# Weighing and adding the even blocks on GpSimd in a mixture of softmaxes

## The chip, the cores and the metric

The kernel runs on one core of a Trainium2 chip. The metric is device time in microseconds (us), the median over the runs of a kernel. Engines are called by the names of the profile: PE is TensorE (PEld its weight loads), DVE is VectorE, ACT is ScalarE, POOL is GpSimd, SP is SyncE, which only issues transfers here.

## The reference

For each of 32·128 = 4096 rows there are 4 heads of 4096 logits and 4 prior values. Each head's logits go through a softmax, the priors go through a softmax over the 4 heads, and the output row is the sum of the four heads' softmaxes, each times its prior:

```
prior_probs = softmax(prior, axis=-1)          # [32, 128, 4]
softmax     = softmax(logits, axis=-1)         # [32, 128, 4, 4096]
mixture     = sum(prior_probs[..., None] * softmax, axis=2)   # [32, 128, 4096]
```

All data are 32-bit floats: 268 MB of logits in, 67 MB of mixture out.

## The kernel before

**Tiles.** A block `n` (of 64) holds 64 output rows. Its 128 partitions are 64 rows times two values of `x`, and a partition holds two heads, `y` = 0 and 1, of 4096 values each: 4 MB in one of five `ring` slots (block n in slot n mod 5). A unit `u` (of 32) is two blocks, the even block `e` = 2u and the odd block `o` = 2u+1, and gives 128 output rows. TensorE's sum goes to four `acc` tiles of PSUM (128 x 1024 each, all of PSUM); the even block's 64 rows are partitions 0 to 63 of `acc`, the odd block's are 64 to 127.

**Steps of a block.** `top(n, y)` (VectorE, L97) finds the negated maximum of each partition's 4096 values. `exp(n, y)` (ScalarE, L104) puts the exponentials in place of the logits and their sum into `dsum`. `weigh(n, y)` takes the reciprocal of the sum (VectorE, L110), and GpSimd multiplies a constant 128 x 64 matrix `mask` (a one where partition p belongs to row p // 2) by reciprocal and prior of the partition (L112): a small weight matrix `wt`. `mix(u, y)` (TensorE, L128) multiplies the exponentials of head half `y` with the weights; the two `x` of a row and, by accumulation in PSUM, the two `y` are summed. Eight column banks of 512, two blocks and two values of `y` make 32 matmuls a unit, which the trace shows as 64 instructions; even and odd block take turns. `drain` (ScalarE, L156) copies `acc` to an output buffer, and `store` (SP, L159) writes 2 MB.

**Order.** It is written out by hand and is the order of each engine's queue. For unit u, with e = 2u, o = 2u+1, the calls are:

```
top(e,0)  weigh(o-2,1)  half(u-1,1)  load(e+3) load(e+4)  top(e,1)
exp(e,0)  exp(e,1)  weigh(e,0)  top(o,0)  weigh(e,1)  top(o,1)
exp(o,0)  weigh(o,0)  drain(u-1)  store(u-1)  half(u,0)  exp(o,1)
```

`half(u, y)` is `mix` in units 0 to 27 (`FINE` = 28). In units 28 to 31 the blocks are cut otherwise: `half` is `pair` (L143), and GpSimd's weight matrices are 128 x 32 (L117). Whole blocks are loaded with L89, block 0 and those of units 28 to 31 in two halves with L94. The two loads of a unit go into the slots of the unit before, so they wait for the last matmul of `half(u-1, 1)`. All loads and stores are issued from SP's queue in this order. The stores of units 27 to 29 are held until unit 31.

Of the kernel before, what the change touches and what calls it, by code (L numbers as in the profile page):

```python
# [9 lines left out]
ALU = mybir.AluOpType  # L10
# [4 lines left out]
def kernel(  # L15
# [3 lines left out]
    prior: bass.AP,  # L19
    out: bass.AP,  # L20
):

# [5 lines left out]
    nc = tc.nc  # L30
# [3 lines left out]
    HP = P // 2  # L34
# [3 lines left out]
    RING = 5  # L38
    BANK = 512
    Q = 4  # L40
    W = V // Q
    HELD = 4
    FINE = U - 4
# [13 lines left out]
    ring = [cpool.tile([P, 2, V], FP32, name=f"ring{i}") for i in range(RING)]  # L57
    obuf = [cpool.tile([P, V], FP32, name=f"obuf{i}") for i in range(2)]
    acc = [psum.tile([P, W], FP32, name=f"acc{i}") for i in range(Q)]
# [4 lines left out]
    mask = cpool.tile([P, HP], FP32, name="mask")  # L64
    mask4 = cpool.tile([P, QP], FP32, name="mask4")
    pt = cpool.tile([P, 2, N], FP32, name="pt")
# [3 lines left out]
    rden = cpool.tile([P, N, 2], FP32, name="rden")  # L70
    wt = [
        [[cpool.tile([P, HP], FP32, name=f"wt{i}{b}{y}") for y in range(2)] for b in range(2)]
        for i in range(2)
    ]
# [33 lines left out]
    def weigh(n, y):  # L108
        w = wt[n // 2 % 2][n % 2][y]
        nc.vector.reciprocal(rden[:, n, y : y + 1], dsum[:, n, y : y + 1])  # L110
        if n < 2 * FINE:
            nc.gpsimd.tensor_scalar(  # L112
                out=w, in0=mask, scalar1=rden[:, n, y : y + 1],
                scalar2=pt[:, y, n : n + 1], op0=ALU.mult, op1=ALU.mult,
            )
        else:
            nc.gpsimd.tensor_scalar(  # L117
                out=w[:, :QP], in0=mask4, scalar1=rden[:, n, y : y + 1],
                scalar2=pt4[:, y, n - 2 * FINE : n - 2 * FINE + 1], op0=ALU.mult, op1=ALU.mult,
            )  # L120

    def mix(u, y):
        for q in range(Q):
            for k in range(W // BANK):
                for b in range(2):
                    n = 2 * u + b
                    c = q * W + k * BANK
                    nc.tensor.matmul(  # L128
                        acc[q][HP * b : HP * (b + 1), k * BANK : (k + 1) * BANK],
                        lhsT=wt[u % 2][b][y],  # L130
                        rhs=ring[n % RING][:, y, c : c + BANK],
                        start=y == 0,
                        stop=y == 1,
                    )

    def pair(u, b):
        n = 2 * u + b
        for q in range(Q):
            for k in range(W // BANK):
                for y in range(2):  # L140
                    g = 2 * b + y
                    c = q * W + k * BANK
                    nc.tensor.matmul(  # L143
                        acc[q][QP * g : QP * (g + 1), k * BANK : (k + 1) * BANK],
                        lhsT=wt[u % 2][b][y][:, :QP],
                        rhs=ring[n % RING][:, y, c : c + BANK],
                        start=True,
                        stop=True,
                        tile_position=(0, QP * g),
                    )  # L150
# [12 lines left out]
    with tc.manual_schedule():  # L163
# [42 lines left out]
        for u in range(U):  # L206
            e, o = 2 * u, 2 * u + 1
            if u:
                top(e, 0)
                weigh(e - 1, 1)  # L210
                half(u - 1, 1)
                load(e + RING - 2)
                load(e + RING - 1)
# [5 lines left out]
            exp(e, 0)  # L219
            exp(e, 1)  # L220
            weigh(e, 0)
            top(o, 0)
            weigh(e, 1)
            if u == LAST:
                for q in range(2):
# [50 lines left out]
```

## Time and profile before

| | us |
|---|---|
| median of 3 runs (787.76 to 787.88) | 787.78 |
| the profiled execution's own time | 787.68 |
| its span, first to last instruction | 786.0 |

| engine | busy us | share of the span |
|---|---|---|
| TensorE matmul | 514.7 | 65% |
| VectorE | 579.0 | 74% |
| ScalarE | 593.9 | 76% |
| GpSimd | 51.7 | 7% |

The 16 DMA engines move 335.97 MB, 427 GB/s over the span. A line of a group in the profile gives the line of code, the engine, the operation, what it writes from what it reads, shapes and count, then total busy us, mean ns of one, and the idle time of the engine ahead of it with what ended it. A line of the timeline gives start and duration in us and, in brackets, the idle time before it and its releaser. "issue" is waiting for nothing that the profile shows.

### The profile page before, as it was taken

To read this page: it belongs to the slowest core of one execution; us is meant where nothing else is said; L and a number is where in the kernel's file an instruction comes from. 1 tells how busy PE (TensorE), PEld (TensorE's weight loads), DVE (VectorE), ACT (ScalarE), POOL (GpSimd) and SP (SyncE) were. 2 spreads that over 40 slices of the span, in tenths; PEclk is the share of its full clock that TensorE was granted. 3 is DMA by queue.
4 is the path that set the end of the run, shared out by engine and by line. 5 is a ranking of instruction groups with operands and counts; after the bars stand their busy time and mean duration, and the time that the engine had idled before them with its cause. 6 is when DMAs were issued, how large, how long until landed. Compare 5 with 4: busy or idle time off the path is not lost.

```text
span 786.0 us, 5580 instructions
## 1 busy us (share of the span) xinstructions
PE 514.7 (65%) x2056; PEld 266.4 (34%) x2056; DVE 579.0 (74%) x270; ACT 593.9 (76%) x382; POOL 51.7 (7%) x141
## 2 busy tenths in 40 slices
PE   0587587555786667865567655676566876575795
PEld 0233344333343333433334333344233443332122
DVE  5888676867768777677776777767877668797982
ACT  3688679777787777887777877778777797797992
POOL 0000000000000000000000000000000000000000
PEclk9998888888977778888899788988778877898888
DMA  9999999999999999999999999999999999999998
GB/s 377 429 436 437 418 439 424 434 435 423 439 430 431 434 429 430 431 434 432 434 424 434 429 435 434 423 435 434 432 433 422 441 433 429 424 429 428 430 428 344
DMA packets 15659, 335.97 MB, mean 427 GB/s; under 512 B 1744, under 2 KB 1808, under 8 KB 2320
## 3 DMA queue, kind: packets, MB, share of 16 engines
q1 hardware_dynamic: 15552, 335.55, 99.6%
q8 instruction: 16, 0.26, 0.1%
q14 instruction: 11, 0.09, 0.0%
q10 hardware_dynamic: 80, 0.07, 0.0%
HBM read 268.50 MB, written 67.11 MB: 427 GB/s over the span
## 4 chain that ended last, share of the span: by engine, by line
DMA 44%; PE 32%; DVE 11%; issue 9%; ACT 2%; POOL 1%; SPq 0%; POOLq 0%; ACTq 0%
DMA ring<-in_logits_dram 44%; PE acc L128 31%; DVE shift L97 10%; PE acc L143 1%; ACT ring L104 1%; POOL wt L112 1%; ACT ring L156 1%; ACT obuf L156 0%; DVE ring L156 0%; DVE rden L110 0%; SPq L94 0%; POOLq L112 0%; ACTq L104 0%
## 5 line engine op out<-in xcount | busy, mean ns | idle before, releaser
L97 DVE TENSOR_REDUCE shift<-ring 128x1 f32<-128x4096 f32 x128 | 563.9, 4409 | 144.0 <-DMA ring<-in_logits_dram 144.0
L128 PE MATMUL acc<-ring,wt 128*64 128x512 f32 x1792 | 454.9, 665 | 221.5 <-issue 212.4
L104 ACT ACTIVATE ring<-ring,shift 128x4096 f32<-128x4096 f32 x128 | 474.9, 3718 | 164.7 <-DVE rden L110 143.8
L128 PEld LDWEIGHTS acc<-ring,wt 128*64 128x64 f32 x1792 | 245.3, 154 | 430.4 <-issue 418.6
L156 ACT COPY obuf<-acc 128x1024 f32<-128x1024 f32 x116 | 108.2, 1014 | 0.0
L112 POOL TENSOR_SCALAR wt<-mask,rden,pt 128x64 f32<-128x64 f32 x112 | 44.0, 393 | 642.3 <-DVE rden L110 618.3
L143 PE MATMUL acc<-ring,wt 128*32 128x512 f32 x256 | 57.9, 668 | 22.1 <-ACT obuf L156 13.6
L110 DVE RECIPROCAL rden<-dsum 128x1 f32<-128x1 f32 x128 | 19.9, 155 | 48.6 <-ACT ring L104 48.6
L143 PEld LDWEIGHTS acc<-ring,wt 128*32 128x32 f32 x256 | 19.4, 121 | 60.5 <-issue 52.7
L104 ACT ACTIVATION_READ_ACCUMULATOR ring<-ring,shift 128x1 f32 x128 | 25.5, 199 | 0.0
L196 PE MATMUL acc<-ident,pr 64*128 64x64 f32 x4 | 1.3, 431 | 19.8 <-DVE pr L192 19.8
L156 ACT COPY ring<-acc 128x1024 f32<-128x1024 f32 (+1 forms) x8 | 7.2, 958 | 8.0 <-PE acc L143 5.0
L117 POOL TENSOR_SCALAR wt<-mask,rden,pt 128x32 f32<-128x32 f32 x16 | 5.9, 367 | 75.5 <-DVE rden L110 71.5
L156 DVE COPY ring<-acc 128x1024 f32<-128x1024 f32 (+1 forms) x5 | 5.5, 1111 | 5.7 <-PE acc L143 5.7
L188 ACT ACTIVATE pr<-pr 64x256 f32<-64x256 f32 x1 | 0.4, 416 | 11.4 <-DVE pr L187 11.4
L196 PEld LDWEIGHTS acc<-ident,pr 64*128 64x128 f32 x4 | 1.0, 316 | 19.8 <-issue 19.8
L188 ACT ACT_TABLE_LOAD x1 | 1.3, 1283 | 1.4 <-PEq L260 1.4
L203 DVE COPY pt<-acc 128x64 f32<-128x64 f32 x2 | 0.5, 226 | 1.2 <-PE acc L196 1.2
L199 PEld LDWEIGHTS acc<-ident,pr 64*128 64x128 f32 x4 | 1.1, 328 | 0.0
L199 PE MATMUL acc<-ident,pr 64*128 64x8 f32 x4 | 1.1, 340 | 0.0
L191 DVE RECIPROCAL pmax<-pmax 64x64 f32<-64x64 f32 x1 | 0.5, 545 | 0.0
L204 DVE COPY pt<-acc 128x8 f32<-128x8 f32 x2 | 0.3, 168 | 0.2
(14 smaller groups left out, 3.8 us busy)
## 6 DMA issues: line engine op xcount, KB each, us to landing
ring<-in_logits_dram SPq DMA_DIRECT2D x55, 4096.0 KB, 25.3
out_dram<-obuf SPq DMA_DIRECT2D x29, 2048.0 KB, 26.9
ring<-in_logits_dram SPq DMA_DIRECT2D x18, 2048.0 KB, 26.3
out_dram<-ring SPq DMA_DIRECT2D x2, 2048.0 KB, 19.0
out_dram<-ring SPq DMA_DIRECT2D x4, 512.0 KB, 6.4
pr<-in_prior_dram ACTq DMA_DIRECT2D x1, 64.0 KB, 7.8
```

Of the source, the lines that this page charges most:

```text
L97: nc.vector.tensor_reduce(out=shift[:, n, y : y + 1], in_=ring[n % RING][:, y], op=ALU.max, axis=AX.X, negate=True,)
L104: nc.scalar.activation(e, e, AF.Exp, bias=shift[:, n, y : y + 1], accum_out=dsum[:, n, y : y + 1])
L110: nc.vector.reciprocal(rden[:, n, y : y + 1], dsum[:, n, y : y + 1])
L112: nc.gpsimd.tensor_scalar(out=w, in0=mask, scalar1=rden[:, n, y : y + 1], scalar2=pt[:, y, n : n + 1], op0=ALU.mult, op1=ALU.mult,)
L117: nc.gpsimd.tensor_scalar(out=w[:, :QP], in0=mask4, scalar1=rden[:, n, y : y + 1], scalar2=pt4[:, y, n - 2 * FINE : n - 2 * FINE + 1], op0 ...
L128: nc.tensor.matmul(acc[q][HP * b : HP * (b + 1), k * BANK : (k + 1) * BANK], lhsT=wt[u % 2][b][y], rhs=ring[n % RING][:, y, c : c + BANK], ...
L143: nc.tensor.matmul(acc[q][QP * g : QP * (g + 1), k * BANK : (k + 1) * BANK], lhsT=wt[u % 2][b][y][:, :QP], rhs=ring[n % RING][:, y, c : c ...
L156: copy(to(u)[:, q * W + f : q * W + t], acc[q][:, f:t])
L188: nc.scalar.activation(pr, pr, AF.Exp)
L191: nc.vector.reciprocal(pmax, pmax)
L196: nc.tensor.matmul(acc[y][:, :N], lhsT=px[:, y], rhs=ident, start=True, stop=True)
L199: nc.tensor.matmul(acc[2 + y][:, :NF], lhsT=p4[:, y], rhs=ident[:, N - NF :], start=True, stop=True)
```

## The change

It concerns units 0 to 27 only. For the two halves of an even block, `weigh` no longer makes weight matrices: GpSimd multiplies the 128 x 4096 exponentials in place by reciprocal and prior, and after `y` = 1 adds the two halves, in place, into the first. In `mix` TensorE then takes the even block once, with `mask` as its weights, in the second half (`y` = 1); the odd block is taken as before in both. The odd block's small weight matrices are made on VectorE, behind the reciprocal. The matmuls of a unit go from 32 to 24 (8 in the first half, 16 in the second).

```diff
     def weigh(n, y):
         w = wt[n // 2 % 2][n % 2][y]
         nc.vector.reciprocal(rden[:, n, y : y + 1], dsum[:, n, y : y + 1])
-        if n < 2 * FINE:
+        if n < 2 * FINE and n % 2 == 0:
+            e = ring[n % RING]
             nc.gpsimd.tensor_scalar(
+                out=e[:, y], in0=e[:, y], scalar1=rden[:, n, y : y + 1],
+                scalar2=pt[:, y, n : n + 1], op0=ALU.mult, op1=ALU.mult,
+            )
+            if y:
+                nc.gpsimd.tensor_add(e[:, 0], e[:, 0], e[:, 1])
+        elif n < 2 * FINE:
+            nc.vector.tensor_scalar(
                 out=w, in0=mask, scalar1=rden[:, n, y : y + 1],
                 scalar2=pt[:, y, n : n + 1], op0=ALU.mult, op1=ALU.mult,
             )
...
     def mix(u, y):
         for q in range(Q):
             for k in range(W // BANK):
-                for b in range(2):
-                    n = 2 * u + b
-                    c = q * W + k * BANK
+                c = q * W + k * BANK
+                if y:
                     nc.tensor.matmul(
-                        acc[q][HP * b : HP * (b + 1), k * BANK : (k + 1) * BANK],
-                        lhsT=wt[u % 2][b][y],
-                        rhs=ring[n % RING][:, y, c : c + BANK],
-                        start=y == 0,
-                        stop=y == 1,
+                        acc[q][:HP, k * BANK : (k + 1) * BANK],
+                        lhsT=mask,
+                        rhs=ring[2 * u % RING][:, 0, c : c + BANK],
+                        start=True,
+                        stop=True,
                     )
+                nc.tensor.matmul(
+                    acc[q][HP:, k * BANK : (k + 1) * BANK],
+                    lhsT=wt[u % 2][1][y],
+                    rhs=ring[(2 * u + 1) % RING][:, y, c : c + BANK],
+                    start=y == 0,
+                    stop=y == 1,
+                )
```

## The prediction

> **What bounds the kernel now.** I read the page's slices first, then the chain that ended last by lines, then the groups.
>
> ```profile
> DMA  9999999999999999999999999999999999999998
> GB/s 377 429 436 437 418 439 424 434 435 423 439 430 431 434 429 430 431 434 432 434 424 434 429 435 434 423 435 434 432 433 422 441 433 429 424 429 428 430 428 344
> DMA ring<-in_logits_dram 44%; PE acc L128 31%; DVE shift L97 10%; PE acc L143 1%; ACT ring L104 1%; POOL wt L112 1%; ACT ring L156 1%; ACT obuf L156 0%; DVE ring L156 0%; DVE rden L110 0%; SPq L94 0%; POOLq L112 0%; ACTq L104 0%
> L97 DVE TENSOR_REDUCE shift<-ring 128x1 f32<-128x4096 f32 x128 | 563.9, 4409 | 144.0 <-DMA ring<-in_logits_dram 144.0
> L104 ACT ACTIVATE ring<-ring,shift 128x4096 f32<-128x4096 f32 x128 | 474.9, 3718 | 164.7 <-DVE rden L110 143.8
> L112 POOL TENSOR_SCALAR wt<-mask,rden,pt 128x64 f32<-128x64 f32 x112 | 44.0, 393 | 642.3 <-DVE rden L110 618.3
> L117 POOL TENSOR_SCALAR wt<-mask,rden,pt 128x32 f32<-128x32 f32 x16 | 5.9, 367 | 75.5 <-DVE rden L110 71.5
> ```
>
> The DMA row is full in every slice but the last, at 418 to 441 GB/s, while no engine is busy over 76%: the transfers set the time. The chain passes through L128 (31%) and L97 (10%) because a load waits for the slot that TensorE frees; whether that wait costs anything is decided by what is still queued then, which comes below. GpSimd's 128 x 64 and 128 x 32 rows will price the new work. Next, two units of the steady state (start:end, busy of each engine, granted clock, DMA share, GB/s):
>
> ```profile
> 282.88:307.13 24.25, 16.61 (x67) 9.13 (x65) 17.84 (x8) 18.62 (x12) 1.57 (x4) 0.79 1.00 432
> 307.13:331.39 24.26, 16.45 (x68) 9.21 (x66) 17.85 (x8) 18.63 (x12) 1.57 (x4) 0.79 1.00 431
> ```
>
> A unit takes 24.25 us: 4.19 + 4.19 + 2.10 MB at 432 GB/s. VectorE is busy 17.85 of it, so it has 6.4 us to spare. Then VectorE's own timeline in that stretch, and SP's:
>
> ```profile
> 287.21 0.15 DVE L110 RECIPROCAL rden<-dsum 128x1 f32<-128x1 f32 x1
> 287.28 4.40 DVE L97 TENSOR_REDUCE shift<-ring 128x1 f32<-128x4096 f32 x1
> 291.60 0.15 DVE L110 RECIPROCAL rden<-dsum 128x1 f32<-128x1 f32 x1
> 292.58 4.42 DVE L97 TENSOR_REDUCE shift<-ring 128x1 f32<-128x4096 f32 x1 [0.83 <-DMA ring<-in_logits_dram]
> 298.55 0.16 DVE L110 RECIPROCAL rden<-dsum 128x1 f32<-128x1 f32 x1 [1.55 <-ACT ring L104]
> 298.63 4.40 DVE L97 TENSOR_REDUCE shift<-ring 128x1 f32<-128x4096 f32 x1
> 302.95 0.15 DVE L110 RECIPROCAL rden<-dsum 128x1 f32<-128x1 f32 x1
> 307.13 4.42 DVE L97 TENSOR_REDUCE shift<-ring 128x1 f32<-128x4096 f32 x1 [4.04 <-DMA ring<-in_logits_dram]
> 311.47 0.15 DVE L110 RECIPROCAL rden<-dsum 128x1 f32<-128x1 f32 x1
> ...
> 308.54 0.86 SPq L89 DMA_DIRECT2D ring<-in_logits_dram  x2
> 319.10 0.34 SPq L159 DMA_DIRECT2D out_dram<-obuf  x1
> ```
>
> 287.21 is the reciprocal of `weigh(e,1)`; I call it R. 291.60 (R+4.39) belongs to `weigh(o,0)`, 292.58 is the next unit's `top(e,0)`, 298.55 (R+11.34) `weigh(o,1)`, 298.63 `top(e,1)`, 307.13 `top(o,0)`, which waits 4.04 us for its data, and 311.47 the next R. VectorE is a chain with room in it, and its room is the wait for data. The loads issued at 308.54 (R+21.3) bring the block that VectorE takes at 331.39. A block is 4.19 MB / 432 GB/s = 9.7 us, so its transfer began at about 321.7: some 12 to 13 us of older transfers were queued when it was issued. A ring slot freed later by less than that costs nothing in the steady state.
>
> **The change, part by part.** The sum is made against the profiled execution: span 786.0, own time 787.68, so 1.7 us lie around the span; the median is 787.78.
>
> *TensorE.* 8 of 32 matmuls go, 16 of 64 instructions of 16.45/64 = 0.257 us: 4.1 us a unit. TensorE idles 7.8 us of each unit, so that is worth nothing by itself.
>
> *GpSimd.* The small weights go (4 x 0.39 us a unit). A 128 x 4096 product: the two rows differ by 26 to 27 ns (mean and median) for 32 elements; with the medians, 393 and 366, that is 0.84 ns an element and 0.34 us fixed, so 0.34 + 4096 x 0.84 ns = 3.78 us, twice (3.66 by the means). The add, A, is in no row. If a second input cost nothing, 3.8 us; two inputs read by turns, 0.34 + 2 x 3.44 = 7.2; three turns with the result's, 10.7. An in-place sum has at least two streams to read, so I take the middle of the upper two, 8.9, and keep 3.8 to 10.7. GpSimd then needs 2 x 3.78 + 8.9 = 16.5 us of 24.25 and does not bind. [...]
>
> *Release of the slots.* In the trace GpSimd starts 0.36 us behind R (287.21 to 287.57). So the product ends at R+4.14, the add runs from R+4.21 (0.07 us between two dependent GpSimd instructions, taken from its setup at the start) to R+4.21+8.9 = R+13.1, and only then can `half(u,1)` start: 32 instructions at 0.21 us (the later pace of 282 to 308) to 0.43 us (the first microseconds of a burst) end at R+20 to R+27, against R+21.3. That is 1 us sooner to 6 us later; the 12 us queue covers it, and without that cover it would be up to 6 us on each of 28 units. At the start there is less cover: the fifth block lands at 52.4, the first release (49.1) brings the sixth at 63.3, 10.9 us later instead of 9.7. There the second half, on a warmed TensorE, ends at 47.6, and at 49.8 if the first ten instructions are at 0.43 us: -1.2 to +0.7 us, once.
>
> *VectorE.* 56 small weights move to it. None is in the trace; between a reciprocal of one column (155 ns) and a copy of 128 x 64 (226 ns), I take 0.2 us: 0.4 us a unit, inside its 6.4. But each sits ahead of a `top` of the next unit, and `weigh(o,0)`'s is ready at R+4.39+0.15 = R+4.55, 0.3 us after GpSimd has begun the add. Does it wait for the add? The trace has VectorE beside GpSimd only in reduces: 287.28 runs over a GpSimd weight and takes 4.40 us, like 298.63. That is a read to one column; no VectorE instruction that writes a tile in SBUF at full rate ran beside GpSimd. So the wait is between 0 and the rest of the add, 13.1 - 4.55 = 8.5 us; a gain is excluded, since nothing there gets shorter. Between the two ends little is likely, since two engines either run side by side or one after the other; I take the whole wait for the forecast and the 0 for the first rival. [...]
>
> With the wait VectorE's chain for one unit is: add ends R+13.1, weight 0.2, `top(e,0)` 4.33 (start to next start), reciprocal and weight 0.35, `top(e,1)` 4.33, reciprocal 0.07, `top(o,0)` 4.33: the next R is 4.21 + A + 13.6 = 17.8 + A = 26.7 us behind R. It exceeds 24.25 as soon as A is over 6.4. The chain is so from unit 0 on, whose next blocks land at 33 and 43, ahead of it. Later data are not late either: released at about R+27, the next block lands 12 us on, and `top(o,0)` wants it 22 us on. ScalarE's `exp(e,1)` ends 0.4 us ahead of the new R.
>
> *The sum.* The first R is at 27.61, the last unit of the change hands over at the R of unit 28, now 697.2. Then: 27.61 + 28 x 26.7 = 775.2, 78 us later. The tail is 786.0 - 697.2 = 88.8 us; its five waits for data (0.27, 3.57, 0.40, 0.41, 0.40, together 5) can go, as the ring is full then, so 84 to 88.8. Span 859 to 864; I take 861, and with 1.7 us around it 863.
>
> **Rivals.**
> *Not slower: VectorE's weight does not wait.* Either the engines do not exclude each other, or the product takes over 4.2 us, so that the weight at R+4.55 is through before the add starts (the margin is 0.3 us, 9% of the product's price). Then the second weight, at R+11.4, would wait at most about 2.5 us for the add, inside VectorE's 6.4. For it: the unslowed reduces, the thin margin. Against it: a constant rate per element over two shapes. DMA stays full, and only the start moves, by -1.2 to +0.7: 786.5 to 788.5, say 787.5.
> *Faster.* The earlier release at the start closes the 1.2 us of idle transfers there: 786.6, which is still within 0.2%; a tail that gains as much again would make 785.4. No row shows that second gain.
> *GpSimd becomes the bound,* whoever waits for whom. If long instructions run at half the rate that the short rows give, 2 x 7.2 + 17.5 = 32 us a unit, 7.8 over 24.25, times 28: about 1000. It decides from A = 16.7 at products of 3.78. The rows come from short instructions only; nothing else speaks for it.
>
> **How the numbers follow.** The waiting weight 0.57, no wait 0.35, a gain at the start 0.04, GpSimd bound 0.04. The heavy chance on the wait is a choice: no row excludes it, and with A anywhere from 6.4 to 10.7 it decides. Its own range: A = 7.2 gives 25.0 us a unit, 27.6 + 700 + 84 + 1.7 = 813; A = 10.7 gives 28.5, 27.6 + 798 + 88.8 + 1.7 = 916. The upper end is for a third turn in full; I stop at A = 9.7 (27.5 a unit, 888) and leave the rest, with GpSimd bound and the gain, outside. Range 786.3 to 888. About 0.2% (1.6 us) is what a measurement of this kernel can tell from no change: faster 0.04, within 0.35, slower 0.61.
>
> **What would show it.** Right: R to R at 26 to 27 us in units 1 to 27; VectorE's weight starting, or ending, with the end of GpSimd's add, and `top(e,0)` behind it; `top` no longer released by DMA; DMA share near 0.9; products of 3.8 us and an add of 8.9. Wrong: VectorE's weight at R+4.6 while the add runs, with `top(o,0)` still released by DMA each 24.25 us; or products over 4.2 us; or GpSimd without idle time.

## The result, and the profile after

The changed kernel takes 853.77 us (median of 5 runs, 853.53 to 854.3), against 787.78 us: a ratio of 1.0838, with a 95% interval of 1.0822 to 1.0854. The prediction was 863 us, with 813 to 916 us for its case and a stated range of 786.3 to 888 us over all cases. The profiled execution has a span of 851.5 us.

In the changed kernel's lines, `top` is L99, the reciprocal L112, GpSimd's product L115, its add L120, VectorE's weight L122, and `mix` L137 (even block, with `mask`) and L144 (odd block). First the page's summary, slices and groups of the changed kernel:

```profile
PE 508.9 (60%) x1608; PEld 167.2 (20%) x1608; DVE 815.1 (96%) x326; ACT 597.2 (70%) x382; POOL 465.8 (55%) x113
DVE  5999999999999999999999999999999999998884
DMA  9979999999999999999999999999999999999998
GB/s 397 419 320 379 406 408 402 392 379 406 406 376 411 373 415 399 387 401 396 401 396 385 411 378 413 402 384 405 391 396 396 394 369 413 398 394 393 429 418 341
L99 DVE TENSOR_REDUCE shift<-ring 128x1 f32<-128x4096 f32 x128 | 562.9, 4405 | 9.9 <-DMA ring<-in_logits_dram 9.9
L115 POOL TENSOR_SCALAR ring<-ring,rden,pt 128x4096 f32<-128x4096 f32 x56 | 210.7, 3763 | 292.5 <-PE acc L144 134.0
L122 DVE TENSOR_SCALAR wt<-mask,rden,pt 128x64 f32<-128x64 f32 x56 | 244.1, 4358 | 5.9
L120 POOL TENSOR_TENSOR ring<-ring 128x4096 f32<-128x4096 f32 x28 | 247.3, 8830 | 2.3
```

VectorE went from 74% to 96% of the span, and is full in every slice from the second up to the tail. Its new work is in L122: 56 small weights of 4.36 us in the mean, 244 us together. The idle time of `top` for data, 144.0 us before, is 9.9 us: VectorE no longer waits for transfers, the transfers wait for VectorE. The DMA row still shows nines, but GB/s has gone from some 430 to mostly 370 to 415. GpSimd's product takes 3.76 us and its add 8.83 us.

One unit on VectorE's timeline:

```profile
291.99 0.16 DVE L112 RECIPROCAL rden<-dsum 128x1 f32<-128x1 f32 x1
292.06 4.40 DVE L99 TENSOR_REDUCE shift<-ring 128x1 f32<-128x4096 f32 x1
296.38 0.16 DVE L112 RECIPROCAL rden<-dsum 128x1 f32<-128x1 f32 x1
296.64 8.41 DVE L122 TENSOR_SCALAR wt<-mask,rden,pt 128x64 f32<-128x64 f32 x1
304.97 4.41 DVE L99 TENSOR_REDUCE shift<-ring 128x1 f32<-128x4096 f32 x1
309.30 0.15 DVE L112 RECIPROCAL rden<-dsum 128x1 f32<-128x1 f32 x1
309.55 0.32 DVE L122 TENSOR_SCALAR wt<-mask,rden,pt 128x64 f32<-128x64 f32 x1
309.78 4.41 DVE L99 TENSOR_REDUCE shift<-ring 128x1 f32<-128x4096 f32 x1
314.11 0.15 DVE L112 RECIPROCAL rden<-dsum 128x1 f32<-128x1 f32 x1
314.18 4.40 DVE L99 TENSOR_REDUCE shift<-ring 128x1 f32<-128x4096 f32 x1
318.50 0.15 DVE L112 RECIPROCAL rden<-dsum 128x1 f32<-128x1 f32 x1
```

and GpSimd's in the same stretch:

```profile
292.31 3.76 POOL L115 TENSOR_SCALAR ring<-ring,rden,pt 128x4096 f32<-128x4096 f32 x1 [0.63 <-DVE rden L112]
296.16 8.84 POOL L120 TENSOR_TENSOR ring<-ring 128x4096 f32<-128x4096 f32 x1
```

R is at 291.99. The add starts at R+4.17. VectorE starts its first weight at R+4.65, 0.48 us later, and holds on to it for 8.41 us, up to 305.05; the add ends at 305.00. The second weight, at 309.55 with GpSimd idle, takes 0.32 us. So the first weight is 8.1 us of waiting, and the next `top` stands behind it. The next R is at 318.50, 26.51 us after this one.

### The profile page after: what moved, and what is told of

The parts are those of the page before. It is cut to its first block, busy times and chain, and to the rows that moved or that the text cites. A ratio compares the mean times of both kernels' runs of the same rounds, so it can differ in the third digit from the quotient of the medians.

```text
span 851.5 us, 4732 instructions
## 1 busy us (share of the span) xinstructions
PE 508.9 (60%) x1608; PEld 167.2 (20%) x1608; DVE 815.1 (96%) x326; ACT 597.2 (70%) x382; POOL 465.8 (55%) x113
## 3 DMA queue, kind: packets, MB, share of 16 engines
q1 hardware_dynamic: 15552, 335.55, 96.7%
## 4 chain that ended last, share of the span: by engine, by line
PE 52%; ACT 24%; issue 11%; DVE 10%; DMA 2%; SPq 0%; ACTq 0%; DVEq 0%
PE acc L144 46%; ACT ring L106 13%; ACT obuf L172 11%; DVE shift L99 7%; PE acc L159 3%; PE acc L137 3%; DMA ring<-in_logits_dram 2%; DVE wt L122 2%; ACT ring L172 0%; DVE ring L172 0%; DVE rden L112 0%; SPq L96 0%; ACTq L172 0%; ACTq L106 0%; DVEq L122 0%
## 5 line engine op out<-in xcount | busy, mean ns | idle before, releaser
L144 PE MATMUL acc<-ring,wt 128*64 128x512 f32 x896 | 450.3, 667 | 300.6 <-issue 281.5
L99 DVE TENSOR_REDUCE shift<-ring 128x1 f32<-128x4096 f32 x128 | 562.9, 4405 | 9.9 <-DMA ring<-in_logits_dram 9.9
L115 POOL TENSOR_SCALAR ring<-ring,rden,pt 128x4096 f32<-128x4096 f32 x56 | 210.7, 3763 | 292.5 <-PE acc L144 134.0
L144 PEld LDWEIGHTS acc<-ring,wt 128*64 128x64 f32 x896 | 134.9, 154 | 602.4 <-issue 600.8
L122 DVE TENSOR_SCALAR wt<-mask,rden,pt 128x64 f32<-128x64 f32 x56 | 244.1, 4358 | 5.9
L120 POOL TENSOR_TENSOR ring<-ring 128x4096 f32<-128x4096 f32 x28 | 247.3, 8830 | 2.3
L137 PE MATMUL acc<-ring,mask 128*64 128x512 f32 x448 | 198.3, 595 | 0.0
L137 PEld LDWEIGHTS acc<-ring,mask 128*64 128x64 f32 x448 | 43.0, 135 | 0.0
L159 PEld LDWEIGHTS acc<-ring,wt 128*32 128x32 f32 x256 | 17.7, 117 | 56.2 <-issue 48.0
L112 DVE RECIPROCAL rden<-dsum 128x1 f32<-128x1 f32 x128 | 19.6, 153 | 9.2 <-ACT ring L106 9.2
```

The source lines that it names most:

```text
L99: nc.vector.tensor_reduce(out=shift[:, n, y : y + 1], in_=ring[n % RING][:, y], op=ALU.max, axis=AX.X, negate=True,)
L115: nc.gpsimd.tensor_scalar(out=e[:, y], in0=e[:, y], scalar1=rden[:, n, y : y + 1], scalar2=pt[:, y, n : n + 1], op0=ALU.mult, op1=ALU.mult,)
L120: nc.gpsimd.tensor_add(e[:, 0], e[:, 0], e[:, 1])
L122: nc.vector.tensor_scalar(out=w, in0=mask, scalar1=rden[:, n, y : y + 1], scalar2=pt[:, y, n : n + 1], op0=ALU.mult, op1=ALU.mult,)
L137: nc.tensor.matmul(acc[q][:HP, k * BANK : (k + 1) * BANK], lhsT=mask, rhs=ring[2 * u % RING][:, 0, c : c + BANK], start=True, stop=True,)
L144: nc.tensor.matmul(acc[q][HP:, k * BANK : (k + 1) * BANK], lhsT=wt[u % 2][1][y], rhs=ring[(2 * u + 1) % RING][:, y, c : c + BANK], start=y ...
```

## The experiments

The theory: VectorE's weight does not run beside a GpSimd instruction, and VectorE waits for the GpSimd instruction that is running. The rivals: the weights are dear on VectorE by themselves; the later release of the slots, or TensorE's one-sided first half, sets the time; GpSimd's 16 us of long instructions in each unit slow the others as such.

**The two parts apart.** `small_on_vector` is the kernel before with one line changed:

```diff
-            nc.gpsimd.tensor_scalar(
+            (nc.vector if n % 2 else nc.gpsimd).tensor_scalar(
                 out=w, in0=mask, scalar1=rden[:, n, y : y + 1],
```

> One part of the change alone: the odd blocks' small weights on VectorE, the even blocks as before (small weights on GpSimd, 32 matmuls a unit). Theory (a VectorE weight waits for the GpSimd instruction that is running): GpSimd's instructions are 0.39 us here, so a weight takes about 0.3 us as it did in the changed kernel when GpSimd was idle, and the time stays at 787.8 within 0.2%. Rival (the weights are dear on VectorE by themselves, 4.4 us in the mean): 28 units lose up to 2 x 4 us of VectorE's chain, about 835.

It takes 787.58 us, a ratio of 0.9998 (0.9988 to 1.0008). A weight on VectorE takes 0.32 us when GpSimd has nothing to do. The weights are not dear.

`all_on_gpsimd` is the changed kernel, with the odd block's weights back on GpSimd behind the add:

```diff
         elif n < 2 * FINE:
-            nc.vector.tensor_scalar(
+            nc.gpsimd.tensor_scalar(
```

> The other part alone: GpSimd weighs and adds the even block and makes the odd block's small weights too, in its queue behind the add; VectorE has none. Theory: VectorE waits for nobody, R to R is 24.25 us again; the weights come at R+13.4, so the loads go out at about R+29 to R+30 instead of R+21.3, which the 12 us of queued transfers cover: 787.8 within 0.3%. Rival (the loss comes from the slots' later release and TensorE's one-sided first half, or from GpSimd's long instructions as such): the release is even later than in the changed kernel, so 850 or more.

It takes 800.47 us, a ratio of 1.0165 (1.0148 to 1.0181): a fifth of the loss, where I had expected none. Two stretches of its trace, from 50 to 70 us and from 110 to 130 us (busy times of PE, PEld, DVE, ACT and POOL, granted clock, DMA share, GB/s):

```profile
50.00:70.00 20.00, 16.27 (x54) 5.39 (x52) 12.28 (x7) 16.03 (x12) 14.27 (x5) 0.91 0.76 313
110.00:130.00 20.00, 15.34 (x48) 5.14 (x48) 14.05 (x8) 14.38 (x11) 12.88 (x6) 0.85 0.99 425
```

the first of them in the kernel before:

```profile
50.00:70.00 20.00, 15.38 (x64) 8.19 (x64) 17.22 (x9) 17.95 (x13) 1.57 (x4) 0.91 1.02 435
```

and one unit in the steady state of `all_on_gpsimd`:

```profile
290.85 4.42 DVE L99 TENSOR_REDUCE shift<-ring 128x1 f32<-128x4096 f32 x1 [4.07 <-DMA ring<-in_logits_dram]
315.12 4.42 DVE L99 TENSOR_REDUCE shift<-ring 128x1 f32<-128x4096 f32 x1 [4.08 <-DMA ring<-in_logits_dram]
300.39 1.18 SPq L91 DMA_DIRECT2D ring<-in_logits_dram  x2
```

One unit there takes as long as expected: `top(o,0)` waits for data at 290.85 and 315.12, 24.27 us apart, though the loads go out at R+29.4 (at 300.39, where the R of that unit is at 270.94) instead of R+21.3. The queue covers that. At the start there is no queue yet: the first two loads are out at 56.9 us instead of 49.5 us, and from 50 to 70 us the engines move 313 GB/s where the kernel before moves 435. Its `top` at 290.85 is 8.0 us behind the same one before (282.88), and 7.1 us of that are there by 95.49 (88.42 before). The R of unit 28 is 10.9 us behind, out of 11.5 us more span; the later part comes in single steps of at most 1.6 us in the steady state, whose cause stays open. The prediction's remark that there is less cover at the start was the right one, and this expectation left it out.

**The form of VectorE's instruction.** `one_port` makes the same weight with two products that also write an accumulator:

```diff
-            nc.vector.tensor_scalar(
-                out=w, in0=mask, scalar1=rden[:, n, y : y + 1],
-                scalar2=pt[:, y, n : n + 1], op0=ALU.mult, op1=ALU.mult,
-            )
+            for src, by in ((mask, rden[:, n, y : y + 1]), (w, pt[:, y, n : n + 1])):
+                nc.vector.tensor_scalar(
+                    out=w, in0=src, scalar1=by, scalar2=None, op0=ALU.mult, op1=ALU.add,
+                    accum_out=sink,
+                )
```

> [...] Theory: no wait, though VectorE has four instructions where it had one (some 0.8 us more for each weight); R to R 24.25 us, 787.8 within 0.3%. Rival (any VectorE instruction that writes a tile waits for GpSimd): 28 x the same 8 us, 853 or more.

It takes 788.87 us, 1.0015 (1.0006 to 1.0024). VectorE's first weight, and GpSimd's add over it:

```profile
291.98 0.28 DVE L124 TENSOR_SCALAR_CACHE_REDUCE wt<-mask,rden 128x64 f32<-128x64 f32 x1
292.18 0.08 DVE L124 DVE_READ_ACCUMULATOR wt<-mask,rden 128x1 f32 x1
292.30 0.28 DVE L124 TENSOR_SCALAR_CACHE_REDUCE wt<-wt,pt 128x64 f32<-128x64 f32 x1
292.50 0.08 DVE L124 DVE_READ_ACCUMULATOR wt<-wt,pt 128x1 f32 x1
292.61 4.42 DVE L100 TENSOR_REDUCE shift<-ring 128x1 f32<-128x4096 f32 x1
```

```profile
291.48 8.90 POOL L121 TENSOR_TENSOR ring<-ring 128x4096 f32<-128x4096 f32 x1
```

The add runs from 291.48 to 300.38, and VectorE's four instructions run inside it, 0.28 us each product and 0.6 us together. GpSimd, TensorE and the order are those of the changed kernel; only the form of the small product differs, and 65 us go. That excludes GpSimd's traffic as such and TensorE's halves as the cause of the loss. The slots' release comes earlier here (the loads go out at 307.60, R+20.3), so it is `all_on_gpsimd` that excludes the release in the steady state: R+29.4 there is later than the changed kernel's R+28.8, and the unit still takes 24.27 us. The run changes two things in the form at once, the accumulator and one scalar in place of two; it does not tell which of them matters. That this form would not wait was an assumption of mine, since no trace up to then had it beside a GpSimd instruction. The traces show 8.41 us for the one form and 0.28 us a product for the other, beside the same add.

**When VectorE is let in.** Four kernels move the add's start or cut it.

`add_after_weight` takes the add out of the even block's `weigh` and puts it behind the odd block's first weight, with a GpSimd copy that waits for that weight:

```diff
+            if y == 0:
+                e = ring[(n - 1) % RING]
+                nc.gpsimd.tensor_copy(sink, w[:, :1])
+                nc.gpsimd.tensor_add(e[:, 0], e[:, 0], e[:, 1])
```

> The changed kernel with the add queued behind a GpSimd copy of one column of VectorE's first weight, so that GpSimd is idle when that weight is made and the add starts about 0.9 us later. This is the first rival of the prediction, made on purpose. Theory: the first weight takes 0.3 us, the second one (ready at about R+11.5) waits for the add's end at R+14, which the spare time of VectorE covers; R to R 24.25, 787.8 within 0.4%. If the loss came from GpSimd's traffic or from the later release: 853 or more.

It takes 787.72 us, 0.9999 (0.9990 to 1.0009). The add now starts at R+5.24 instead of R+4.17, and both weights are seen on VectorE:

```profile
292.06 0.32 DVE L121 TENSOR_SCALAR wt<-mask,rden,pt 128x64 f32<-128x64 f32 x1
298.97 2.64 DVE L121 TENSOR_SCALAR wt<-mask,rden,pt 128x64 f32<-128x64 f32 x1
```

The second one waits 2.3 us for the add, up to 301.6, inside VectorE's spare time. So 1.1 us later for the add is worth 66 us: the first rival of the prediction, made on purpose.

`add_in_four` cuts the add into four instructions of 1024 columns, with no wait between them:

```diff
-                nc.gpsimd.tensor_add(e[:, 0], e[:, 0], e[:, 1])
+                for c in range(0, V, V // 4):
+                    d = slice(c, c + V // 4)
+                    nc.gpsimd.tensor_add(e[:, 0, d], e[:, 0, d], e[:, 1, d])
```

> The changed kernel with the add cut into four instructions of 1024 columns, queued one behind the other without a wait between them. Theory as the prediction had it (the wait is for the one running instruction): the weight waits at most for the end of a quarter, 2.2 us, and the time is 788 to 790. Theory as corrected by the run with the memset (VectorE waits until GpSimd's run of queued instructions ends): the whole add again, 853 to 856.

One run: 789.42 us, beside 787.7. The weight waits for the end of the running quarter:

```profile
293.81 1.91 DVE L124 TENSOR_SCALAR wt<-mask,rden,pt 128x64 f32<-128x64 f32 x1
300.72 1.96 DVE L124 TENSOR_SCALAR wt<-mask,rden,pt 128x64 f32<-128x64 f32 x1
```

```profile
293.33 9.30 POOL L122 TENSOR_TENSOR ring<-ring 128x1024 f32<-128x1024 f32 x4
```

293.33 + 9.30/4 = 295.66, and the weight that started at 293.81 ends at 295.72, while three quarters are still queued. The wait is for one instruction, and the corrected theory, which I had formed after the run with the memset (below), that VectorE waits for the whole run of queued instructions, fell here.

`product_add_by_turns` cuts the second product too, product and add by turns in quarters:

```diff
+            for c in range(0, V, V // 4 if y else V):
+                d = slice(c, c + (V // 4 if y else V))
+                nc.gpsimd.tensor_scalar(
+                    out=e[:, y, d], in0=e[:, y, d], scalar1=rden[:, n, y : y + 1],
+                    scalar2=pt[:, y, n : n + 1], op0=ALU.mult, op1=ALU.mult,
+                )
+                if y:
+                    nc.gpsimd.tensor_add(e[:, 0, d], e[:, 0, d], e[:, 1, d])
```

> The changed kernel with the second product and the add cut into quarters that take turns, so that each add has to wait for the product ahead of it (some 0.07 us in which GpSimd is idle). The cut costs GpSimd some 6 x 0.3 us of fixed time. If VectorE is let in at such a gap, a weight waits 3.5 us at most and the time is 788 to 792. If it waits until GpSimd's queue is empty, R to R grows by the cut's cost to 28 or 28.5 us: 890 to 910.

One run: 787.81 us. The weights take 0.69 us in the median and 1.30 at most: one that starts at 292.26, inside a product of 1.19 us from 291.57, ends at 292.81 with it.

`add_later` had come before these, and had misled me: a memset of an unused tile between product and add.

```diff
             if y:
+                nc.gpsimd.memset(pad, 0.0)      # pad: 128 x 768
                 nc.gpsimd.tensor_add(e[:, 0], e[:, 0], e[:, 1])
```

> The changed kernel with one more GpSimd instruction: a memset of an unused 128x768 tile (about 0.75 us) between the second product and the add, so that the add starts behind R+4.65, where VectorE's weight is ready. Theory with the margin of the first rival of the prediction: the weight waits at most for the end of the memset and is let in before the add; only the second weight meets the add and waits some 2.5 us, which VectorE has to spare: more work for GpSimd, yet 787.8 to 790. If VectorE is not let in between two queued GpSimd instructions, or if GpSimd's traffic as such is the cause: 853 or a little more.

868.99 us, 1.1033 (1.1017 to 1.1049): slower than the changed kernel, so the theory's 787.8 to 790 missed, and the rival's "853 or a little more" was nearer. The add starts at R+4.73, 0.56 us later than in the changed kernel, and R to R is 27.07 us, 0.56 us more (between two first weights, 302.44 to 329.51). VectorE's weight and GpSimd around it:

```profile
302.44 8.97 DVE L124 TENSOR_SCALAR wt<-mask,rden,pt 128x64 f32<-128x64 f32 x1
```

```profile
301.82 0.74 POOL L121 MEMSET pad<- 128x768 f32 x1
302.52 8.84 POOL L122 TENSOR_TENSOR ring<-ring 128x4096 f32<-128x4096 f32 x1
```

The weight starts 0.08 us before the add does and still has to wait for all of it. Is it the memset, or did the weight come too late? `add_later_reading` has a product by constants on a 128x512 tile in the memset's place:

```diff
-                nc.gpsimd.memset(pad, 0.0)
+                nc.gpsimd.tensor_scalar(
+                    out=pad, in0=pad, scalar1=1.0, scalar2=1.0, op0=ALU.mult, op1=ALU.mult
+                )
```

> As the run with the memset, but the instruction between product and add reads and writes its 128x512 tile (a product by constants, about 0.8 us) where the memset only wrote. The run with the add in four pieces let VectorE in at the end of a piece. If that holds for any GpSimd instruction that reads SBUF, the weight waits some 0.4 us here and the time is 788 to 790, and the memset is the exception. If VectorE is let in only between two adds, or only where GpSimd waits: 28 x 0.8 us over the changed kernel, about 870.

One run: 861.95 us. It told nothing of the question, since this instruction took only 0.63 us: the add started at 297.00 and the weight at 297.01. `add_much_later_reading` has the same on 128x1536:

> The same with the product by constants on 128x1536 (about 1.5 us) in the memset's place; with 128x512 the weight came 0.01 us behind the add's start. If VectorE is let in between any two GpSimd instructions: 788 to 790. If only between two adds: about 895.

One run: 787.90 us, beside 787.79. The instruction takes 1.47 us, and the weight at 292.35 gets in at its end, 293.22. It is through at 293.27 and does not wait for the add, whose record starts at 293.19:

```profile
292.35 0.92 DVE L126 TENSOR_SCALAR wt<-mask,rden,pt 128x64 f32<-128x64 f32 x1
```

```profile
291.75 1.47 POOL L121 TENSOR_SCALAR pad<-pad 128x1536 f32<-128x1536 f32 x1
293.19 8.90 POOL L124 TENSOR_TENSOR ring<-ring 128x4096 f32<-128x4096 f32 x1
```

So one more GpSimd instruction of 1.5 us makes the changed kernel 66 us faster. The memset's twin was to be longer as well:

> The memset before the add made longer (128x1536, about 1.35 us, R+4.0 to R+5.4), so that VectorE's weight, ready at R+4.65, comes 0.7 us before the add can start; with 128x768 it came 0.08 us before. If VectorE is let in between any two GpSimd instructions and had only come too late: the weight waits 0.7 us at most and the time is 788 to 790. If it is not let in behind an instruction that only writes: the add follows at once, R to R is 26.5 + 1.3 = 27.8 us, about 890.

The kernel that ran had a 128x512 tile instead of that (its memset takes 0.52 us), so that the add began (300.00) before the weight (300.14): 862.76 us in one run, which again says only that the weight came late. Whether VectorE gets in behind a GpSimd instruction that only writes, or whether 0.08 us was too short a lead, stays open.

**The weight on another engine.** `small_on_scalar` makes it on ScalarE:

```diff
+            nc.scalar.activation(w, mask, AF.Copy, scale=rden[:, n, y : y + 1])
+            nc.scalar.activation(w, w, AF.Copy, scale=pt[:, y, n : n + 1])
```

> GpSimd weighs and adds the even block as in the changed kernel; the odd block's weights are made on ScalarE by two scaled copies (some 0.3 us each, four a unit, of 5.6 us that ScalarE has to spare). VectorE has no weight, and GpSimd none behind its add, so the first release comes at about 48 to 50 us as in the kernel before. Theory: 787.8 within 0.3%. Rival (a GpSimd that is busy 16 us of a unit slows the kernel in itself): 800 or more.

It takes 788.09 us, 1.0005 (0.9995 to 1.0014), with GpSimd busy 16.4 us of each 24.25 us unit. A busy GpSimd costs nothing here.

**The chain's formula.** `add_three_quarters` adds 3072 of the 4096 columns; its even rows lack the second pair of heads in the last quarter:

```diff
-                nc.gpsimd.tensor_add(e[:, 0], e[:, 0], e[:, 1])
+                nc.gpsimd.tensor_add(
+                    e[:, 0, : 3 * V // 4], e[:, 0, : 3 * V // 4], e[:, 1, : 3 * V // 4]
+                )
```

> The changed kernel with the add over 3072 of the 4096 columns only (the last quarter of the even rows leaves the second pair of heads out). This tests the chain's formula, R to R = 17.7 us + A with the measured 8.83 us add, and its threshold. With 2.1 ns a column (from the 1024-column adds, 2.36 us) A is 6.7 us, so R to R is 24.3 to 24.4, just over the transfers' 24.25: 27.3 + 28 x 24.35 + 82 + 2 = 793 us (788 to 796). A loss in proportion to GpSimd's add time would be three quarters of 66 us: 837.

794.33 us, 1.0086 (1.0069 to 1.0103). The add takes 6.67 us and R to R is 24.35 us (294.89 to 319.23 is 24.34): a quarter less of the add takes away nine tenths of the loss, as a threshold does and a proportion does not.

No version beat the kernel before: `small_on_vector`, `add_after_weight`, `small_on_scalar` and, in one run each, the two others at 787.8 and 787.9 tie with it, because all of them stand at the transfers' 24.25 us a unit; `one_port` and `add_in_four` are 1.1 and 1.7 us above it.

## Why the prediction was right

*The bound and the point from which it decides.* Right: VectorE's spare 6.4 us decide, and with the weight's wait its chain is longer than the transfers' 24.25 us. R to R was 26.5 us against 26.7 predicted; with A = 8.83 us, the rest of the chain is 17.7 us against 17.8. The run with three quarters of the add stands at A = 6.67, just above the threshold of 6.4, and just above the transfers. These readings, more than the time alone, speak for the mechanism: the stated range held the 787.5 us of the rival without a wait as well.

*GpSimd's prices.* 3.78 us for a product was 3.76; 8.9 us for the add was 8.83. The add's price was the middle of two ends that the rows of short one-input instructions gave; the ends (7.2 and 10.7) would have made 813 or 916 us. That the middle was within 0.1 us was luck: 2.1 ns a column is 2.5 times the product's 0.84 ns, which is neither the two turns nor the three of the prediction's accounts.

*The wait.* Taken in full, 8.5 us against 8.1 measured (8.41 less 0.31 for the weight itself). It was the one step that no row of the kernel before could decide, and taking it in full was a choice, at a chance of 0.57. `one_port` shows that it is the form of the instruction, `add_in_four` and `add_much_later_reading` that it lasts until the running GpSimd instruction ends. The margin was put at 0.3 us and was 0.48 us, as VectorE's weight starts 0.26 us behind the start of its reciprocal, not 0.15.

Two readings under this step were wrong. The reduce at 298.63, which stands there as the one without GpSimd, runs over a GpSimd weight too (298.91); those that ran alone, at 292.58 and 307.13, took 4.42 us, so reduces are unslowed all the same. And the kernel before does have VectorE beside GpSimd in something other than a reduce: at its end VectorE copies `acc` to a tile in SBUF while GpSimd makes a weight.

```profile
766.22 2.33 DVE L156 COPY ring<-acc 128x1024 f32<-128x1024 f32 x2
766.50 0.37 POOL L117 TENSOR_SCALAR wt<-mask,rden,pt 128x32 f32<-128x32 f32 x1 [4.72 <-DVE rden L110]
```

Neither waits: GpSimd's weight takes its usual 0.37 us in the middle of the first copy, and the two copies take 2.33 us together, where one without GpSimd takes 1.22 us (776.40). This row speaks for the rival without a wait, and the prediction did not weigh it. It does not settle the step either: this copy reads PSUM and the weight reads SBUF, and no run shows whether that matters; only the runs show which forms wait.

*The sum.* R of unit 28 was put at 775.2 and was at 769.26: 28 x 0.2 us of the chain make 5.6 of the 5.9 us. The tail was put at 84 to 88.8 us and took 851.5 - 769.26 = 82.2: 6.6 us less, where the waits for data were to give at most 5. They are gone, but waits for ScalarE grew in their place (three of 2.43 us, against 2.05, 1.41 and 1.91), so up to `weigh(o,0)` of unit 31 (766.13 before, 834.56 now) only 3.7 us were saved; the other 2.9 us lie behind it, 2.5 of them after VectorE's last copy, where the last stores landed 3.7 us after their issue in the median instead of 6.4. Together these are the 9 us between 863 and 854.

*What was wrong without harm.* TensorE was to save 4.1 us a unit. It did not: 16.02 us busy against 16.45. The one-sided first half has the time from 305.15 to 312.82, 7.7 us, to itself (the granted clock is 0.50 for its first 4 us), and 13 of its 16 instructions start in it; by their count the last three run beside the first even ones of the second half, which is through at 320.8, 8.0 us on. At the same granted clock of 1.00 a one-sided instruction follows the one ahead after 0.43 us, and a pair of an even and an odd one follows the pair ahead after 0.43 us as well. The kernel before has its weight loads two at a time, 0.43 us from one two to the next (297.62, 298.05, 298.48), so two instructions share each 0.43 us, and 0.257 us was not what dropping one of the two saves. And the DMA share was to fall to 0.9: it stayed at 0.96 to 0.98 in the steady state, at 390 to 396 GB/s instead of 432. The reading "418 to 441 GB/s" for every slice of the kernel before but the last misses its first one, 377.

*The release.* The loads went out at R+28.8 (320.79), later than the R+20 to R+27 of the case without a wait, since VectorE's first weight let TensorE start its first half only at R+13.2 (305.15). That cost nothing in the changed kernel, whose VectorE is later still: the 9.9 us that `top` waits for data all lie before 23 us. That a queue covers such a delay in the steady state but not at the start is shown by `all_on_gpsimd`.

## What to carry to other kernels

Before an instruction is moved to an engine because that engine is idle, look at what else will run at that moment, and at which form the instruction has: here VectorE's small instruction waited in one form for all that was left of GpSimd's long one (8.1 us), and everything queued behind it waited too; in another form it took 0.28 us a product beside the same add. Where the small one cannot change its engine or form, cut the long one into pieces, or start it later; here 1 us of later start, or four pieces, gave back 64 to 66 us. Where transfers set the time, look at what is still queued before a stall is priced: in `all_on_gpsimd` the queue covered loads that went out 8 us later in the steady state (24.27 us a unit), but not at the start (313 GB/s from 50 to 70 us instead of 435), where no queue had built up.

## What the runs showed that I had not expected

VectorE's wait ends with the GpSimd instruction (an add, a product; for a memset it stays open), even where the next one is queued with no wait between: a weight got in between two quarters of the add at 295.7 us. The cut itself costs little: a 1024-column add takes 2.36 us, four of them 9.30 us against 8.83 us for the whole.

Two matmuls whose results go to the two halves of `acc` ran side by side: these weight loads of the changed kernel, one for each instruction, are 0.43 us apart in the one-sided half at the granted clock of 1.00,

```profile
310.67 0.14 PEld L144 LDWEIGHTS acc<-ring,wt 128*64 128x64 f32 x1 [0.29 <-issue]
311.10 0.14 PEld L144 LDWEIGHTS acc<-ring,wt 128*64 128x64 f32 x1 [0.29 <-issue]
311.53 0.14 PEld L144 LDWEIGHTS acc<-ring,wt 128*64 128x64 f32 x1 [0.29 <-issue]
```

while, once the even block's matmuls join, they come in pairs 0.43 us apart (313.24 and 313.30, then 313.67 and 313.73):

```profile
313.24 0.59 PE L144 MATMUL acc<-ring,wt 128*64 128x512 f32 x1
313.30 0.59 PE L137 MATMUL acc<-ring,mask 128*64 128x512 f32 x1
313.67 0.59 PE L144 MATMUL acc<-ring,wt 128*64 128x512 f32 x1
313.73 0.59 PE L137 MATMUL acc<-ring,mask 128*64 128x512 f32 x1
```

So taking the even block's matmuls out of the first half saved TensorE next to nothing.

A DMA share near 1 did not mean that the transfers were the bound. In the changed kernel queue q1's packets took 96.7% of 851.5 us, 823 us, and in the kernel before 99.6% of 786.0 us, 783 us, for the same 335.55 MB. The share stayed up while the rate fell from 427 to 395 GB/s; the idle time of `top` for data, 144.0 us against 9.9, told the two apart.
